# Expert-value tiles 70 to 127 multiplied in three products of split halves

## The chip, the cores and the metric

One Trainium2 chip, one of its cores. The kernel is launched once and computes the whole output. The metric is device time in microseconds (us). Before the change the median of three runs is 2919.87 us (2919.39 to 2923.93).

## The reference

Two transformer blocks run one after the other on 512 tokens of width 1024, all in float32. The first has sliding-window attention, spatial gating and a mixture of 32 experts; the second has a convolution, forgetting attention and a feed-forward layer that picks, for each token, 16 experts out of 16384 in each of 8 heads. The change touches that last layer alone:

```python
u = peer_u[ec]                                   # 128 chosen rows of each token
a = gelu(einsum("ckd,cd->ck", u, hc)) * gc       # a factor for each
vv = peer_v[ec]
out = einsum("ck,ckd->cd", a, vv)                # weighted sum of rows of peer_v
```

`peer_u` and `peer_v` have 16384 rows of 1024 numbers each. The result is added to the tokens, and a last norm follows.

## The kernel before, in words

`peer` (from line 1463) computes this layer in two ways at once, beside each other.

**Gathered half.** For the first 256 tokens (two tiles of 128, `GT`) the chosen rows are fetched one expert slot at a time: `row` (line 1795) has GpSimd issue an indirect DMA that brings one row of 4 KB to each of the 128 partitions (line 1797). There are twelve such buffers (`rtile`). `dots` (line 1804, VectorE) multiplies a fetched row of `peer_u` with the token. `v_sum` adds up four fetched row sets of `peer_v` at a time on TensorE, by weights in `wz` (copied on ScalarE at line 1821; matmuls at line 1825). One such sum stands for four gathers, and it frees four of the twelve buffers. After the 32 sums of a token tile `last_norm` (lines 1834 to 1841) adds the tokens, norms and stores; it runs on VectorE and ScalarE.

**Dense half.** For the other 256 tokens (`DT`) every expert is computed. `u_tile` multiplies one of 128 tiles of `peer_u` (128 experts) with all 256 tokens and writes gelu of it as a slot of 128x256 factors. `gates` (lines 1731 to 1770) builds the gate of each expert and token out of one-hot tiles in batches of 8 tokens, on VectorE (lines 1759 to 1764) and TensorE (line 1748), and multiplies the slots by it on VectorE (line 1752, one instruction for each stretch of slots that lies in one tile). It runs in three parts: experts' tiles 0 to 15, 16 to 79 and 80 to 127. The last part is spread over the steps of V tiles 34 to 79. `v_tile` (line 1772) loads one tile of `peer_v` (512 KB, four buffers, issued by SyncE at line 1490) and multiplies it by its slot: four float32 matmuls at line 1776, for two token tiles and two halves of 512 columns, each recorded as two matmuls. All 128 V tiles add into four banks of PSUM.

There are 94 slots (`NS`); slot i holds tiles i and i+94. The first 50 (`NA`) lie in `big`, the other 44 in `big2`, which is made when U tile 50 is reached. After V tile 69 the slots 50 to 69 hold nothing that is needed any more, since no tile above 127 comes.

**Order.** The loop at line 1886 goes through a list of 256 steps: U tiles 0 to 93, then V and U tiles in turn, then V tiles 34 to 127 alone. After each step it emits a share of the gate batches and, by `fill`, about 2.3 gathers with the sums that go with them. Each engine executes its instructions in the order in which they are emitted.

Elsewhere in the kernel matmuls are made of three products: `split` (line 81) lets ScalarE copy a float32 tile into a rounded half `hi` of type float32r (line 83), and VectorE subtract it for `lo` (line 84); `mm3` (lines 136 to 138) then multiplies hi by hi, hi by lo and lo by hi. Both are used unchanged by the change.

Of the kernel before, what the change touches and what calls it, by code (L numbers as in the profile page):

```python
# [8 lines left out]
F32 = mybir.dt.float32  # L9
F32R = mybir.dt.float32r  # L10
# [10 lines left out]
S, D, NT, KD = 512, 1024, 4, 8  # L21
# [10 lines left out]
class Kern:  # L32
# [1430 lines left out]
    def peer(self):  # L1463
        nc, tc, A = self.nc, self.tc, self.A
        tt, ts, stt = nc.vector.tensor_tensor, nc.vector.tensor_scalar, nc.vector.scalar_tensor_tensor
        act = nc.scalar.activation
        GT, DT, DW = (0, 1), (2, 3), 256
        NS, NA = 94, 50
        parts = [0, 16, 80, 128]
        TB = 8  # L1470
        GS = 32768.0
        with ExitStack() as ctx:
            pb = ctx.enter_context(tc.tile_pool(name="pb", bufs=1, reuse_waits="tile"))
# [4 lines left out]
            def pu(shape=(128, 512)):  # L1478
                return pp.tile(list(shape), F32, tag="u", name=self.nm("pu"), bufs=2)

            def pw(shape=(128, 512)):
                return pp.tile(list(shape), F32, tag="w", name=self.nm("pw"), bufs=4)
# [4 lines left out]
            def load(src, shape):  # L1487

                raw = wp.tile([128] + shape, F32, tag="raw", name=self.nm("raw"))
                nc.sync.dma_start(raw[:], src)  # L1490
                return raw
# [9 lines left out]
            gp = [pb.tile([128, DW], F16, name=f"gp{j}") for j in range(2)]  # L1501
            hd = [pb.tile([128, 4, DW], F32, name=f"hd{j}") for j in range(2)]
            lctx = ctx.enter_context(ExitStack())
            lv = lctx.enter_context(tc.tile_pool(name="plv", bufs=1, reuse_waits="tile"))
            v = [lv.tile([128, 8, 2, 16], F32, name=f"pv{t}") for t in range(NT)]
            ix = [lv.tile([128, 8, 2, 16], U32, name=f"pix{t}") for t in range(NT)]
# [101 lines left out]
            with ExitStack() as c2:  # L1608
# [12 lines left out]
                for t in range(NT):  # L1621
                    tb = slice(t * 128, t * 128 + 128)
                    for j in range(2):
                        x = self.xn[t][j]
# [48 lines left out]
            def picks():  # L1673
# [9 lines left out]
                for t in DT:  # L1683
# [10 lines left out]
                    gT = wk.tile([128, 128], F32, tag="gT", name=self.nm("gT"))  # L1694
                    ts(gT[:], p[:, 2, :], GS, None, op0=OP.mult)
                    nc.vector.tensor_copy(gp[0][:, sl], gT[:])
# [9 lines left out]
            big = [bp.tile([128, NA, DW], F32, name="big")]  # L1706

            def slots(n0, n1):

                while n0 < n1:  # L1710
                    i = n0 % NS
                    b, i, w = (0, i, NA) if i < NA else (1, i - NA, NS - NA)
                    m = min(n1, n0 + w - i)
                    yield n0, m, big[b], i
                    n0 = m

            def slot(n):
                _, _, b, i = next(slots(n, n + 1))
                return b[:, i, :]

            def u_tile(n):

                p = pu()
                raw = load(A["peer_uT"][n].rearrange("p (k e) -> p k e", k=8), [8, 128])
                for k in range(KD):
                    self.u_last = nc.tensor.matmul(p[:, :DW], raw[:, k, :], hd[k // 4][:, k % 4, :], start=k == 0,  # L1726
                                                   stop=k == KD - 1)
                self.gelu = act(slot(n), p[:, :DW], AF.Gelu_apprx_tanh)  # L1728
                self.pace = self.u_last

            def gates(n0, n1, psum):

                w, g = n1 - n0, TB // 2

                def by2(x, t0, w):
                    return x[:, t0:t0 + TB].rearrange("p (g i) -> p g i", i=2)[:, :, None, :].to_broadcast([128, g, w, 2])

                made = []  # L1740

                def products():
                    t0, o2, og = made.pop(0)
                    p = psum([128, TB, w])
                    with tc.issue_after(self.pace.ins):
                        for i in range(TB):
                            for j in range(2):
                                nc.tensor.matmul(p[:, i, :], o2[:, i // 2, :, i % 2], og[j][:, i // 2, :, i % 2], start=j == 0,  # L1748
                                                 stop=j == 1)
                    for n, m, b, i in slots(n0, n1):  # L1750
                        b = b[:, i:i + m - n, t0:t0 + TB]
                        stt(b, p[:, :, n - n0:m - n0].rearrange("p t n -> p n t"), 1.0 / GS, b, op0=OP.mult, op1=OP.mult)  # L1752

                for t0 in range(0, DW, TB):
                    if len(made) == 2:
                        products()
                    o2 = ga.tile([128, g, 128, 2], F16, tag="o2", name=self.nm("o2"), bufs=3)
                    eq = ga.tile([128, g, w, 2], F16, tag="eq", name=self.nm("eq"))
                    tt(o2[:], io[:, None].to_broadcast([128, g, 128, 2]), by2(e2b, t0, 128), op=OP.is_equal)
                    tt(eq[:], io[:, None, n0:n1].to_broadcast([128, g, w, 2]), by2(e1b, t0, w), op=OP.is_equal)  # L1760
                    og = []
                    for j in range(2):
                        o = ga.tile([128, g, w, 2], F16, tag=f"og{j}", name=self.nm("og"), bufs=3)
                        tt(o[:], eq[:], by2(gp[j], t0, w), op=OP.mult)
                        og.append(o)
                    made.append((t0, o2, og))
                    yield
                while made:
                    products()
                    yield  # L1770

            def v_tile(n, acc):
                raw = load(A["peer_v_2"][n * 128:n * 128 + 128, :], [D])
                a = slot(n)
                for t, c in itertools.product(range(2), range(2)):
                    self.pace = nc.tensor.matmul(acc[t][c][:], a[:, t * 128:t * 128 + 128], raw[:, c * 512:c * 512 + 512],  # L1776
                                                 start=n == 0, stop=n == 127)

            def rest_of_big():
                lctx.close()  # L1780
                bq = ctx.enter_context(tc.tile_pool(name="pbig2", bufs=1, reuse_waits="tile"))
                big.append(bq.tile([128, NS - NA, DW], F32, name="big2"))


            ga_t = [ga.tile([128, 128], F32, name=f"ga{t}") for t in GT]
# [78 lines left out]
            def fill(n):  # L1864
                with tc.issue_after(self.pace.ins):
                    while n > 0:
                        k = next(units, None)
                        if k is None:
                            return 0.0
                        n -= k  # L1870
                return n
# [11 lines left out]
            acc, gt, todo, room = None, None, 0, 0.0  # L1883
            nbatch = DW // TB

            for j, (kind, n) in enumerate(seq):
                if kind == "v" and n == 0:
                    acc = [[pw() for _ in range(2)] for _ in range(2)]
                if kind == "v" and n in parts and gt is not None:
                    for _ in gt:  # L1890
                        pass
                    gt = None
                if kind == "u":
                    if n == NA:
                        for _ in picks:
                            pass
                        rest_of_big()
                    if n % 3:
                        next(picks, None)
                    u_tile(n)  # L1900
                else:
                    v_tile(n, acc)
                if gt is not None:
                    todo += rate
                    while todo >= 1:
                        todo -= 1
                        next(gt, None)
                if (kind, n) in start:
                    i = start[kind, n]
                    gt, todo = gates(parts[i], parts[i + 1], pu if i else pw), 0.0  # L1910

                    rest = seq.index(("v", parts[i])) - j - 1
                    rate = (nbatch + 2) / (rest - 1)

                room = fill(room + (1.4 if acc is None and n < NA else 2.3))
# [90 lines left out]
```

## Time and profile before

| | |
|---|---|
| median of three runs | 2919.87 us |
| profiled execution | 2930.82 us |
| its span | 2929.1 us |
| TensorE busy | 2717.2 us (93%) |
| VectorE busy | 1848.5 us (63%) |
| ScalarE busy | 1019.7 us (35%) |
| GpSimd busy | 723.5 us (25%) |
| moved by DMA | 752.10 MB, mean 257 GB/s |

The profiled execution takes 1.7 us more than its span, and 10.95 us more than the median. Shares of busy time are means over the whole span, and its stages have different limits, so the stretch that the change touches has to be read by itself, by windows cut at its own steps. Times in the rows are microseconds from the span's start; PE is TensorE, PEld its weight loads, DVE VectorE, ACT ScalarE, POOL GpSimd, SP SyncE. The "PEclk" column is the granted TensorE clock as a share of 2.4 GHz. "DMA share" is the mean share in which the core's 16 DMA engines had packets under way; packets overlap, so it can pass 1.

### The profile page before, as it was taken

The page shows a single profiled execution, that of the slowest core. Times are in us where ns is not written, and L with a number is a line of the kernel's source. Part 1 is how long each engine was busy: PE and PEld are TensorE (multiplying, and loading weights), DVE is VectorE, ACT ScalarE, POOL GpSimd, SP SyncE. Part 2 cuts the span into 40 slices and gives each one's busy share as a digit, 9 for nine tenths or more (in the row PEclk, how much of TensorE's full clock was granted, in tenths as well). Part 3 has the DMA queues.
Part 4 walks back from the last instruction along what each step waited for, and adds up shares of the span by engine and source line. Part 5 has one row for each costly group of instructions (what it writes and reads, how often), then busy time and mean ns, then how long its engine had stood idle before and what let it go on. Part 6 is the DMA issues. An engine that isn't in the chain of part 4 may idle for free.

```text
span 2929.1 us, 38343 instructions
## 1 busy us (share of the span) xinstructions
PE 2717.2 (93%) x13730; PEld 1907.3 (65%) x13730; DVE 1848.5 (63%) x3907; ACT 1019.7 (35%) x1672; POOL 723.5 (25%) x679
## 2 busy tenths in 40 slices
PE   7999969999999879999999889989989898699998
PEld 4776757777777667766678778877745554244333
DVE  5562569998888858998535399968557522452001
ACT  5442348777777653445633332200100000000000
POOL 1000050000000110101000343566543444444440
PEclk9999979999999989999999999999999999899999
DMA  7226568989999842322222348899988899999995
GB/s 258 87 86 215 206 212 324 355 319 354 351 351 348 317 148 86 108 72 66 89 91 94 119 166 284 335 409 409 360 326 318 327 362 350 324 355 360 369 375 184
DMA packets 228689, 752.10 MB, mean 257 GB/s; under 512 B 28160, under 2 KB 28448, under 8 KB 228496
## 3 DMA queue, kind: packets, MB, share of 16 engines
q1 hardware_dynamic: 145936, 458.69, 43.7%
q0 software_dynamic: 81984, 289.89, 27.1%
q8 instruction: 109, 1.79, 0.3%
q10 hardware_dynamic: 576, 1.05, 0.1%
q14 instruction: 84, 0.69, 0.1%
HBM read 736.90 MB, written 16.81 MB: 257 GB/s over the span
## 4 chain that ended last, share of the span: by engine, by line
PE 40%; DVE 9%; DMA 7%; issue 6%; POOL 2%; ACT 1%; DVEq 0%; another core or an unknown queue 0%; POOLq 0%; SPq 0%; ACTq 0%
PE pw L1776 12%; DMA u<-in_peer_u_dram,ei 6%; PE pu L1726 4%; PE pm L136 4%; PE pm L138 4%; PE pm L137 4%; PE pr L1825 3%; POOL u L1797 2%; DVE u L1804 2%; PE pa L1305 2%; DVE cv L1236 1%; PE pu L1748 1%; PE po L1334 1%; PE pw L138 1%; PE pw L136 1%
## 5 line engine op out<-in xcount | busy, mean ns | idle before, releaser
L84 DVE TENSOR_TENSOR lo<-raw,hi 128x1024 fp32r<-128x1024 f32 (+1 forms) x580 | 624.4, 1107 | 234.3 <-ACT hi L83 214.0
L83 ACT ACTIVATE hi<-raw 128x1024 fp32r<-128x1024 f32 (+1 forms) x600 | 556.9, 952 | 445.1 <-PE pm L137 197.0
L1804 DVE CUSTOM_DVE_ANT_0 u<-u,h 128x1024 f32<-128x1024 f32 x256 | 311.3, 1226 | 305.3 <-DMA u<-in_peer_u_dram,ei 258.7
L1726 PE MATMUL pu<-hd,raw 128*128 128x256 f32 x2048 | 474.1, 390 | 17.4 <-issue 8.3
L1776 PE MATMUL pw<-raw,big 128*128 128x512 f32 x1024 | 471.4, 609 | 6.7 <-DVE big L1752 6.7
L1726 PEld LDWEIGHTS pu<-hd,raw 128*128 128x128 f32 x2048 | 394.3, 195 | 94.9 <-issue 30.2
L1776 PEld LDWEIGHTS pw<-raw,big 128*128 128x128 f32 x1024 | 191.2, 193 | 252.7 <-issue 244.0
L1797 POOL DMA_INDIRECT u<-in_peer_v_dram,eT x256 | 259.2, 1012 | 378.5 <-DVE ga L1804 210.1
L1797 POOL DMA_INDIRECT u<-in_peer_u_dram,ei x256 | 288.4, 1126 | 204.7 <-issue 54.3
L1728 ACT ACTIVATE big<-pu 128x256 f32<-128x256 f32 x128 | 48.9, 384 | 492.6 <-PE pu L1726 430.8
L137 PE MATMUL pm<-lo,xth 128*128 128x512 f32 x512 | 204.8, 400 | 6.5 <-DVE lo L84 6.5
L136 PE MATMUL pm<-hi,xth 128*128 128x512 f32 x512 | 202.1, 395 | 0.0
L138 PE MATMUL pm<-hi,xtl 128*128 128x512 f32 x512 | 201.3, 393 | 0.0
L1236 DVE SCALAR_TENSOR_TENSOR cv<-z,cols,cv 128x496 f32<-128x496 f32 (+27 forms) x240 | 167.2, 735 | 0.5
L905 POOL DMA_INDIRECT yd<-y,idx x16 | 27.6, 1726 | 540.1 <-DVE y L1009 536.6
L138 PE MATMUL pm<-hT,lo 128*128 128x512 f32 x384 | 151.2, 395 | 0.0
L136 PE MATMUL pm<-hT,hi 128*128 128x512 f32 x384 | 151.1, 394 | 0.0
L137 PE MATMUL pm<-hT,hi 128*128 128x512 f32 x384 | 151.0, 393 | 0.0
L1821 ACT ACTIVATE wz<-aT 128x4 f32<-128x4 f32 x64 | 12.8, 209 | 396.9 <-PE pr L1825 396.8
L1825 PE MATMUL pr<-u,wz 128*32 128x512 f32 x1024 | 126.4, 612 | 8.3 <-DMA u<-in_peer_v_dram,eT 8.3
L137 PEld LDWEIGHTS pm<-lo,xth 128*128 128x128 f32 x512 | 96.4, 188 | 40.3 <-DVE lo L84 19.7
L1748 PEld LDWEIGHTS <-o 128*128 128x128 f16 x1536 | 55.0, 98 | 87.5 <-DVE big L1752 43.2
(575 smaller groups left out, 4323.8 us busy)
## 6 DMA issues: line engine op xcount, KB each, us to landing
raw<-in_w_gate_dram SPq DMA_DIRECT2D x128, 512.0 KB
raw<-in_w_up_dram SPq DMA_DIRECT2D x128, 512.0 KB
raw<-in_w_down_dram SPq DMA_DIRECT2D x128, 512.0 KB
raw<-in_peer_uT_dram SPq DMA_DIRECT2D x128, 512.0 KB
raw<-in_peer_v_dram SPq DMA_DIRECT2D x128, 512.0 KB
raw<-in_w_in_dram SPq DMA_DIRECT2D x104, 256.0 KB
wa<-in_w_ada_dram SPq DMA_DIRECT2D x48, 512.0 KB
raw<-in_w_in_dram SPq DMA_DIRECT2D x28, 512.0 KB
```

The costliest lines, as they stand in the source:

```text
L83: return (self.nc.scalar.activation(hi, src, AF.Copy), (eng or self.nc.vector).tensor_tensor(lo, src, hi.bitcast(F32), op=OP.subtract))
L84: (eng or self.nc.vector).tensor_tensor(lo, src, hi.bitcast(F32), op=OP.subtract))
L136: mm(ps, a[0], b[0], start=first, stop=False, **kw)
L137: mm(ps, a[0], b[1], start=False, stop=False, **kw)
L138: return mm(ps, a[1], b[0], start=False, stop=last, **kw)
L1236: stt(a[:, d:], z[:, :512 - d], self.col("conv_w", k * 31 + j), a[:, d:], op0=OP.mult, op1=OP.add)
L1726: self.u_last = nc.tensor.matmul(p[:, :DW], raw[:, k, :], hd[k // 4][:, k % 4, :], start=k == 0, stop=k == KD - 1)
L1748: nc.tensor.matmul(p[:, i, :], o2[:, i // 2, :, i % 2], og[j][:, i // 2, :, i % 2], start=j == 0, stop=j == 1)
L1776: self.pace = nc.tensor.matmul(acc[t][c][:], a[:, t * 128:t * 128 + 128], raw[:, c * 512:c * 512 + 512], start=n == 0, stop=n == 127)
L1797: nc.gpsimd.indirect_dma_start(out=u[:], out_offset=None, in_=A[src], in_offset=bass.IndirectOffsetOnAxis(ap=idx, axis=0))
L1804: nc.vector.tensor_tensor_reduce(u[:], u[:], h3[t][:], scale=1.0, scalar=0.0, op0=OP.mult, op1=OP.add, accum_out=ga_t[t][:, s:s + 1])
L1825: m = nc.tensor.matmul(acc[c][32 * g:32 * g + 32, :], w[:, g, 31 - r:63 - r], us[g][:, c * 512:c * 512 + 512], start=r == 0, stop=r == 31, ...
```

## The change

V tiles below 70 are multiplied as before. From tile 70 on, `v_split` loads the tile, splits it into `vh` and `vl` (128x1024 each) and the slot of factors into `ah` and `al` (128x256 each), and `v_three` multiplies them with `mm3`: four times three float32r matmuls. The split of tile n+1 is emitted ahead of the matmuls of tile n. The four halves have two buffers each, 20 KB in each partition altogether, in a pool that is opened when tile 70 is reached, where slots 50 to 69 lay: `big2` becomes two tiles, slots 50 to 69 and slots 70 to 93 (`big3`), and the first is closed then. `slots` therefore knows three stretches instead of two. The check that all gates of a part are done comes one tile earlier from tile 70 on.

```diff
+        V3 = 70
+            self.b2ctx = ctx.enter_context(ExitStack())
...
-                    b, i, w = (0, i, NA) if i < NA else (1, i - NA, NS - NA)
+                    b = 0 if i < NA else 1 if i < V3 else 2
+                    i, w = i - (0, NA, V3)[b], (NA, V3 - NA, NS - V3)[b]
...
+            def v_split(n):
+
+                raw = load(A["peer_v_2"][n * 128:n * 128 + 128, :], [D])
+                vh, vl, ah, al = [self.vp.tile([128, w], F32R, tag=x, name=self.nm(x), bufs=2)[:] for x, w in (
+                    ("vh", D), ("vl", D), ("ah", DW), ("al", DW))]
+                self.split(ah, al, slot(n))
+                self.split(vh, vl, raw[:])
+                return vh, vl, ah, al
+
+            def v_three(n, acc, x):
+                vh, vl, ah, al = x
+                for t, c in itertools.product(range(2), range(2)):
+                    e, d = slice(t * 128, t * 128 + 128), slice(c * 512, c * 512 + 512)
+                    self.pace = self.mm3(acc[t][c][:], (ah[:, e], al[:, e]), (vh[:, d], vl[:, d]), n == 0, n == 127)
...
-                bq = ctx.enter_context(tc.tile_pool(name="pbig2", bufs=1, reuse_waits="tile"))
-                big.append(bq.tile([128, NS - NA, DW], F32, name="big2"))
+                bq = ctx.enter_context(tc.tile_pool(name="pbig3", bufs=1, reuse_waits="tile"))
+                b3 = bq.tile([128, NS - V3, DW], F32, name="big3")
+                bq = self.b2ctx.enter_context(tc.tile_pool(name="pbig2", bufs=1, reuse_waits="tile"))
+                big.extend([bq.tile([128, V3 - NA, DW], F32, name="big2"), b3])
...
-                if kind == "v" and n in parts and gt is not None:
+
+                if kind == "v" and n + (n >= V3) in parts and gt is not None:
...
+                elif n < V3:
+                    v_tile(n, acc)
                 else:
-                    v_tile(n, acc)
+                    if n == V3:
+                        self.b2ctx.close()
+                        self.vp = ctx.enter_context(tc.tile_pool(name="pv3", bufs=1, reuse_waits="tile"))
+                        nx = v_split(n)
+                    cur, nx = nx, v_split(n + 1) if n < 127 else None
+                    v_three(n, acc, cur)
```

## Rows read from the trace of the kernel before

**Rows 1.** The page: busy time of each engine, its share of the span, instructions.

```profile
PE 2717.2 (93%) x13730; PEld 1907.3 (65%) x13730; DVE 1848.5 (63%) x3907; ACT 1019.7 (35%) x1672; POOL 723.5 (25%) x679
```

**Rows 2.** Windows cut at V tiles 0, 16, 70, 80, 115, end.

```profile
core 0: us, PE busy (x) PEld busy (x) DVE busy (x) ACT busy (x) POOL busy (x), PEclk, DMA share, GB/s
...
2125.64:2312.09 186.45, 157.41 (x1058) 96.85 (x1056) 123.32 (x276) 8.43 (x26) 74.53 (x76) 0.95 0.88 316
...
2663.92:2713.60 49.68, 49.68 (x295) 20.56 (x291) 12.27 (x35) 1.05 (x5) 19.72 (x21) 1.00 0.97 363
2713.60:2874.80 161.20, 161.20 (x604) 59.90 (x600) 0.64 (x1) 3.57 (x17) 70.90 (x78) 1.00 0.98 370
2874.80:2919.70 44.90, 44.90 (x108) 19.68 (x104) 4.01 (x9) 3.19 (x10) 0.00 (x0) 1.00 0.37 126
```

**Rows 3.** Groups by line on TensorE, window 2713.60 to 2874.80.

```profile
L1776 PE MATMUL pw<-raw,big 128*128 128x512 f32 x280 | 125.5, 600 | 0.0
L1825 PE MATMUL pr<-u,wz 128*32 128x512 f32 x324 | 39.1, 598 | 0.0
```

**Rows 4.** TensorE's timeline: the last sum of gathered rows, then V tiles alone.

```profile
2872.95 1.92 PE L1825 MATMUL pr<-u,wz 128*32 128x512 f32 x16
2874.80 44.90 PE L1776 MATMUL pw<-raw,big 128*128 128x512 f32 x104
```

**Rows 5.** TensorE's timeline, experts: first and last of 24 float32r matmuls.

```profile
904.59 0.39 PE L138 MATMUL pm<-hi,xtl 128*128 128x512 f32 x1
...
909.86 0.39 PE L137 MATMUL pm<-lo,xth 128*128 128x512 f32 x1
```

**Rows 6.** Groups by form: splits (600-1000 us), gelu, gate multiplies (2125-2312 us).

```profile
L83 ACT ACTIVATE hi<-raw 128x1024 fp32r<-128x1024 f32 x262 | 263.0, 1053 | 32.6 <-PE pm L138 26.2 <-DMA raw<-in_w_down_dram 4.4 <-DMA raw<-in_w_up_dram 0.7
...
L84 DVE TENSOR_TENSOR lo<-raw,hi 128x1024 fp32r<-128x1024 f32 x263 | 306.9, 1220 | 30.3 <-ACT hi L83 29.2
...
L1728 ACT ACTIVATE big<-pu 128x256 f32<-128x256 f32 x40 | 15.4, 385 | 243.8 <-PE pu L1726 222.7 <-issue 16.3 <-PE pw L1748 4.8
...
L1752 DVE SCALAR_TENSOR_TENSOR big<-pu,big 128x272 f32<-128x272 f32 x31 | 13.4, 434 | 1.7 <-PE pu L1748 1.6
...
L1752 DVE SCALAR_TENSOR_TENSOR big<-pu,big 128x240 f32<-128x240 f32 x31 | 12.3, 397 | 0.0
```

**Rows 7.** DMA, 2663.92 to 2864 us; GpSimd's timeline: the last gather.

```profile
DMA packets 20367, 74.24 MB, mean 371 GB/s; under 512 B 2268, under 2 KB 2268, under 8 KB 20356
...
2852.11 0.94 POOL L1797 DMA_INDIRECT u<-in_peer_v_dram,eT  x1 [0.30 <-issue]
```

**Rows 8.** DMA of GpSimd's queue, 2864 to 2866 us: packets, MB, share.

```profile
q0 software_dynamic: 55, 0.17, 21.4%
```

**Rows 9.** Windows: dot products with U tiles, sums (columns of rows 2).

```profile
1900.00:2050.00 150.00, 135.17 (x846) 116.47 (x845) 111.94 (x241) 13.94 (x40) 103.66 (x80) 0.94 1.03 409
2713.60:2852.00 138.40, 138.40 (x517) 51.59 (x514) 0.00 (x0) 3.57 (x17) 66.71 (x71) 1.00 0.99 371
```

**Rows 10.** Timelines of VectorE and ScalarE: the norm behind the last sum.

```profile
2874.16 1.47 DVE L1837 TENSOR_TENSOR xe<-xe,pr 128x512 f32<-128x512 f32 x2 [161.69 <-PE pr L1825]
...
2877.16 1.41 DVE L1840 SCALAR_TENSOR_TENSOR xo<-xe,rs,gf 128x512 f32<-128x512 f32 x2
...
2876.61 0.30 ACT L203 ACTIVATE rs<-ss,eps 128x1 f32<-128x1 f32 x1 [0.23 <-DVE ss L202]
```

**Rows 11.** VectorE's timeline: the dense norm's second add.

```profile
2918.03 0.69 DVE L1837 TENSOR_TENSOR xe<-xe,pw 128x512 f32<-128x512 f32 x1 [0.17 <-PE pw L1776]
```

**Rows 12.** Gathers (2713-2852, 2100-2350, 1900-2050 us by form; whole span by line).

```profile
L1797 POOL DMA_INDIRECT u<-in_peer_v_dram,eT x71 | 66.7, 940 | 75.8 <-PE pr L1825 56.0 <-issue 14.5 <-PE pw L1776 5.3
...
L1797 POOL DMA_INDIRECT u<-in_peer_v_dram,eT x55 | 56.9, 1034 | 105.4 <-DVE ga L1804 99.5 <-DVE eq L1760 2.7 <-issue 2.3
...
L1797 POOL DMA_INDIRECT u<-in_peer_u_dram,ei x69 | 92.2, 1336 | 32.2 <-issue 16.4 <-DMA u<-in_peer_u_dram,ei 12.8 <-DVE og L1764 3.0
...
L1797 POOL DMA_INDIRECT u<-in_peer_v_dram,eT x256: 935/939/1982, 2018.6 to 2852.1; - x128
```

## Prediction, made before the changed kernel was run

> **What bounds the kernel now.** The page's first table shows TensorE busy for 2717.2 us of the span [rows 1]: the engine to relieve, but a share over the whole span says nothing of one stage. So the second view is windows cut at the steps that the change touches [rows 2]. V tile 70 starts at 2663.92 us. In the 49.68 us up to tile 80, in the 161.20 us up to tile 115 and in the 44.90 us of the last 13 tiles alone TensorE is busy all the time at full clock, 2.4 GHz: in these 255.8 us every microsecond taken from TensorE could come off the end. The same rows carry the warning. In the first two windows the DMA share is 0.97 and 0.98, with 363 and 370 GB/s; only behind the last sum does it fall to 0.37. I call these two windows the mixed stretch (210.9 us) and the third the tail.
>
> The third view, groups by line, shows what fills the mixed stretch: V tiles (280 records, eight a tile, so 35 tiles from tile 80 on) and sums of gathered rows (324 records, 16 a sum) [rows 3]. With the ten tiles before, it holds 45 V tiles and, by the sums that the trace counts there, 26 sums. Each sum waits for four gathers, and each V tile for its 512 KB. So a shorter TensorE helps in the mixed stretch only as far as transfers can follow; in the tail it helps in full.
>
> **The matmuls.** The tail takes 44.90 us for 13 tiles [rows 4], 3.45 us each. A new tile has twelve float32r matmuls. In the experts 24 such matmuls of the same shape, bound by nothing else, start from 904.59 to 909.86 us [rows 5]: 5.27 us for 23 steps, 0.229 us each. Twelve make 2.75 us, and a tile saves 0.70 us. Neither row holds a wait, so no range is needed here. The Trainium skill, page "FP8 and Floating Point Precision", section "TensorE Precision Notes", counts four passes for a true float32 matmul, by which three products would take three quarters, 2.59 us as an estimate: 0.11 us a tile less than measured here for the same instructions, some 1.4 us in the tail.
>
> **The splits.** Each tile adds on ScalarE a copy of 128x1024 (1.053 us) and one of 128x256 (0.385 us, the gelu of that shape), on VectorE a subtraction of 128x1024 (1.220 us) and one of 128x256 (0.397 us by the nearest row, 128x240) [rows 6]. That is 1.44 and 1.62 us per tile; beside a tile of 2.75 us it fits, and both engines are nearly idle in the mixed stretch (ScalarE 4.62 us, VectorE 12.91 us in 210.9 us, rows 2 added). The halves have two buffers, so the split of tile n+2 waits until tile n is multiplied, and has only tile n+1's matmuls as cover. The way from the end of tile n to `vl` of n+2 is 0.385 + 1.053 + 1.220 us and three handoffs of at most 0.23 us, the one that the norm's row shows [rows 10]: between 2.66 and 3.35 us. The second product of n+2 needs it 2.75 + 0.23 = 2.98 us after. Two tiles then take that way plus 2.52 us of products, so the step is between 2.75 (covered) and 2.94 us; I take 2.85. Where a sum of 1.85 us (2872.95 to 2874.80 [rows 4]) stands between, it is covered. Tiles 70 to 79 have gate work ahead of the subtraction on VectorE, 12.27 us for ten tiles [rows 2]; if the cover is gone, a tile loses up to 1.2 us, and tiles with a sum beside them lose nothing. I take 2 us for all ten, between 0 and 12.
>
> **The switch at tile 70.** The new buffers lie where slots 50 to 69 were, so the first split waits for tile 69's matmuls, and nothing covers it: 2.66 us, up to 3.35. The gathers run on meanwhile. A pair of loads is not added: SyncE loads the same tiles through the same four buffers, now freed by the splits, a tile earlier.
>
> **The norm behind the last sum.** `last_norm` for the second token tile stands in VectorE's and ScalarE's queues ahead of the split of tile 116. VectorE is in it from 2874.16 until 2878.57 us, 4.6 us behind the sum's last product near 2874.0; ScalarE until 2876.91 [rows 10]. The subtractions need another 1.6 us, so `vl` of tile 116 comes some 6 us after the sum, and TensorE, with one tile ready (2.75 us and a product of 0.23), stands still for 3 us; now it has only V tiles there and waits for nobody. Between 0 (if that norm is emitted a step later) and 6; I take 3.
>
> **The mixed stretch, as TensorE sees it.** 210.9 us less 45 times 0.70 (31.5), plus 2.7 for the switch and 2 for the gates: 184.1 us.
>
> **The mixed stretch, as transfers see it.** From tile 70's start to 2864 us 74.24 MB move at 371 GB/s; the last gather is issued at 2852.11 [rows 7] and q0's packets have thinned out to 0.17 MB in the 2 us from 2864 on [rows 8]. Its sum starts at 2872.95, so gathers now run 9 us ahead of TensorE. That lead is used up first if TensorE becomes faster than its rows. What is unknown is the rate when the queues never run dry. The trace has it at 409 GB/s, with 1.03 of the engines' share, for 150 us in which the same gathers ran beside tiles of the same size; in the sums' stretch it is 371 at 0.99 [rows 9]. So the ends are 371 (the engines have no more to give with this mix) and 409. I take 400, nearer the upper one: it has the same two queues and sizes, and waiting packets are what the change makes. 74.24 MB then take 185.6 us, and with 1 us for the landing and 1.85 for the last sum the stretch is 188.5 us, longer than TensorE's 184.1: transfers set its end, and it saves 22.4 us. At 409 it is 184.4 us (26.5 saved), at 371 it is 203.0 us (7.9 saved).
>
> **The tail.** Of 13 tiles the last counts half, because the norm's first adds start at 2918.03 us, within it [rows 11]: 12.5 times 0.60 (3.45 less 2.85) is 7.5 us, less 3 for the norm: 4.5. What follows the last tile is unchanged.
>
> **Earlier.** Tiles 16 to 79 now lie in three pieces, so each of 32 gate batches has three multiplies on VectorE where it had two. They take 434 + 397 ns for 272 and 240 numbers a partition [rows 6]; for 272, 160 and 80 the same line gives about 434 + 320 + 240, 0.16 us more, 5.2 us in all. In that window VectorE works 123.32 of 186.45 us [rows 2], and the rest, waits for rows, covers most. I take 1, between 0 and 5.
>
> **The sum.** 22.4 + 4.5 - 1 = 25.9 us: 2930.82 becomes 2904.9 for the profiled execution, and against the median, 10.95 us below it, 2919.87 becomes 2894.0. A measurement of this kernel can tell about 0.2% (5.8 us) from no change.
>
> **The rivals.**
> *The transfers give nothing more.* At 371 GB/s the mixed stretch saves 7.9 us, the whole 7.9 + 4.5 - 1 = 11.4: 2908.5. For it: the share is 0.99 already. Against it: 409 for 150 us. The Trainium skill's "DMA: Bandwidth & Descriptors", section "Where 436 GB/s comes from", puts the HBM side at about 358 GB/s per core as what binds loads; the trace disagrees, with 409 and 371. Chance 0.17.
> *TensorE stays the bound and the covers hold.* At 409 GB/s, with no gate, norm or handoff stall: 31.5 - 2.7 saved in the stretch is more than transfers allow, so 26.5 + 12.5 times 0.70 = 35.3: 2884.6. Chance 0.08.
> *Little or nothing is left.* 371 GB/s, the norm's stall at 6 us, the gates' extra work uncovered: 7.9 + 7.5 - 6 - 5 = 4.4, within 0.2%: 2915.5. Chance 0.08.
> *Slower: the subtractions hold up GpSimd's gathers.* A gather takes 0.940 us with VectorE idle, 1.034 and 1.336 us where VectorE runs two-operand products and other work, at most 1.982 [rows 12], plus 0.30 us between two [rows 7]. A sum has 210.9/26 = 8.11 us now; four gathers pass that from 1.73 us a gather on. If every gather met a subtraction and took 1.98, four would take 9.1 us, 26 sums 26 us more, and with the tail 26 - 4.5 + 1 = 22.5 slower: 2942. Against it: VectorE is busy 112 of 150 us where the mean is 1.336 [rows 9, 12], and the new work is 1.6 us in some 4. The Trainium skill, "SBUF — State Buffer", section "Who interferes with whom", says that a VectorE instruction with two SBUF inputs contends with a GpSimd instruction that reads SBUF; the subtraction is one, and the trace shows a loss of 0.09 to 0.4 us a gather beside such work. Chance 0.07.
> The forecast itself has 0.60. That the products are not the cheap ones can be ruled out: the type and shape are those of rows 5.
>
> **The numbers.** 2894 us. The range reaches from a little under the second rival (2884.6) to the first with its earlier gate work uncovered too (2908.5 + 4): 2882 to 2912; what it leaves out is the third and the fourth, and some of the second. Faster by over 0.2%: the forecast, the first two rivals, 0.85, less a little of the first's upper end: 0.82. Within 0.2%: 0.10. Slower: 0.08. TensorE's clock is in these: where it was busy for 157.41 of 186.45 us it had 0.95 [rows 2], and a wait of a few per cent in the mixed stretch may cost some of that.
>
> **What would show it.** The windows after should have V tiles of twelve matmuls, 2.75 to 2.95 us in the tail; a mixed stretch near 188 us with DMA at 400 GB/s and TensorE waiting for gathered rows or raw tiles; one gap of 2.7 us at tile 70 and one of 3 us after the last sum. Wrong would be: waits of TensorE for `vl` at every tile, a rate still at 371 with a share near 1 (first rival), or gathers of over 1.7 us on GpSimd (the slower one).

## The result and the profile after

The changed kernel takes 2890.66 us (median of four runs, 2888.25 to 2899.49) against 2921.77 us before (four runs, the three from above and one more): a ratio of 0.9899, with a 95% interval from 0.9876 to 0.9922. That is 31 us less, where 26 were forecast, inside the range of 2882 to 2912.

The two profiled executions differ by more: their spans are 2929.1 and 2886.5 us, 42.6 us apart. So the first thing to read is where in the span the difference lies. These are windows of the changed kernel, cut at the same steps as [rows 2] (V tiles 70, 80, 115 and the last one's end; same columns):

```profile
2653.14:2696.57 43.43, 43.37 (x329) 27.18 (x329) 28.88 (x56) 15.93 (x27) 20.73 (x20) 1.00 1.02 400
2696.57:2839.20 142.63, 139.26 (x745) 85.80 (x741) 57.61 (x70) 51.45 (x87) 79.37 (x78) 0.99 1.03 409
2839.20:2876.78 37.58, 36.55 (x160) 28.96 (x156) 23.33 (x31) 17.78 (x31) 0.00 (x0) 1.00 0.54 191
```

The mixed stretch went from 49.68 + 161.20 = 210.88 us to 43.43 + 142.63 = 186.06 us, the tail from 44.90 to 37.58 us. Together that is 32.1 us, near the 31 us between the medians. The other 10 us lie ahead of tile 70, which starts at 2653.14 us for 2663.92: experiment 1 shows that single executions scatter there by more than that, so they can't be put down to the change. Two columns changed with the time: transfers went from 363 and 370 to 400 and 409 GB/s, with the engines' share at 1.02 and 1.03; and TensorE, busy without a break before, has 3.4 us of idle time among sums and tiles. All that it waited for on the way, by the view of waits (waiter, what ended it: us in total, times, the longest):

```profile
PE pr L1845 <- DMA u<-in_peer_v_dram,eT: 3.4, 3, 2.3
PE pw L136 <- ACT vh L83: 1.1, 1, 1.1
PE pw L137 <- DVE vl L84: 1.0, 1, 1.0
```

Three waits for gathered rows, one for `vh` (the switch at tile 70) and one for `vl` (the norm behind the last sum). In 58 tiles there is no wait on a split's round but those two.

### The profile page after: what moved, and what is told of

It reads as the page before. It is cut to its first block, busy times and chain, and to the rows that moved or that the text cites. A ratio compares the mean times of both kernels' runs of the same rounds, so it can differ in the third digit from the quotient of the medians.

```text
span 2886.5 us, 39245 instructions
## 1 busy us (share of the span) xinstructions
PE 2676.6 (93%) x13962; PEld 1946.1 (67%) x13962; DVE 1943.7 (67%) x4055; ACT 1099.6 (38%) x1788; POOL 738.7 (26%) x679
## 4 chain that ended last, share of the span: by engine, by line
PE 40%; DVE 9%; DMA 7%; issue 5%; POOL 2%; ACT 1%; DVEq 0%; POOLq 0%; ACTq 0%; SPq 0%
PE pu L1729 5%; PE pw L1794 5%; DMA u<-in_peer_u_dram,ei 5%; PE pm L136 4%; PE pm L138 4%; PE pm L137 4%; PE pr L1845 4%; PE pw L136 2%; PE pw L137 2%; PE pw L138 2%; DVE u L1824 2%; POOL u L1817 2%; DMA u<-in_peer_v_dram,eT 2%; PE pa L1305 2%; DVE cv L1236 1%
## 5 line engine op out<-in xcount | busy, mean ns | idle before, releaser
L1817 POOL DMA_INDIRECT u<-in_peer_v_dram,eT x256 | 272.9, 1066 | 346.1 <-DVE ga L1824 203.9
L1794 PE MATMUL pw<-raw,big 128*128 128x512 f32 x560 | 262.8, 614 | 3.2 <-DVE big L1755 3.2
L1794 PEld LDWEIGHTS pw<-raw,big 128*128 128x128 f32 x560 | 105.1, 195 | 131.2 <-issue 126.1
L136 PEld LDWEIGHTS pm<-hi,xth 128*128 128x128 f32 x512 | 96.3, 188 | 21.1 <-ACT xth L83 0.2
```

The source lines that it names most:

```text
L136: mm(ps, a[0], b[0], start=first, stop=False, **kw)
L1817: nc.gpsimd.indirect_dma_start(out=u[:], out_offset=None, in_=A[src], in_offset=bass.IndirectOffsetOnAxis(ap=idx, axis=0))
```

## The experiments

The first four take the change apart. Beside each of the eleven, the kernel before ran on the same chip.

**1. Only the three pieces.** All V tiles keep the float32 matmuls; the slots lie in three tiles.

```diff
-                elif n < V3:
+                elif n < 128:
                     v_tile(n, acc)
...
             while next(units, None) is not None:
                 pass
+            self.b2ctx.close()
```

> The slots lie in three tiles and the pool stays open, but all 128 V tiles are multiplied as before, so nothing is left of the change but a third gate multiply in each of 32 batches. My theory of the early part: 0 to 5.2 us slower than before, about 1 us. Rival, from the two profiles (tile 70 starts 10.8 us earlier after the change): the new layout itself gains there, and this kernel is some 10 us faster than before.

Measured: 2920.89 us (ten runs) against 2922.99, ratio 0.9995, interval 0.9982 to 1.0008. The third piece costs nothing that can be measured, and the 10 us that the rival gives the layout lie outside the interval (some 5 us faster to 2 us slower). Yet in its profiled execution the time from V tile 0 to tile 70 was 521.0 us, where the first profile of the kernel before had 538.3 (row one, this kernel; row two, the one before; windows):

```profile
2120.10:2641.13 521.03, 469.07 (x2546) 252.56 (x2545) 261.77 (x601) 23.54 (x76) 241.26 (x241) 0.96 0.94 348
```

```profile
2125.64:2663.92 538.28, 474.72 (x2547) 256.25 (x2545) 260.91 (x569) 23.58 (x76) 238.87 (x241) 0.95 0.92 338
```

Two executions with the same work there, but for 32 gate multiplies more on VectorE in the quicker one, lie 17 us apart. What makes one of them slower stays open. A difference of that size ahead of tile 70 between two single profiles therefore says nothing; the mixed stretch, by contrast, has 210.97 and 210.88 us.

**2 and 3. Only the tail, only the mixed stretch.**

```diff
# experiment 2
-                elif n < V3:
+                elif n < 115:
                     v_tile(n, acc)
...
-                    if n == V3:
+                    if n == 115:
# experiment 3
-                elif n < V3:
+                elif n < V3 or n >= 115:
                     v_tile(n, acc)
...
-                    cur, nx = nx, v_split(n + 1) if n < 127 else None
+                    cur, nx = nx, v_split(n + 1) if n < 114 else None
```

> Only tiles 115 to 127, behind the last sum, are multiplied in three products. If the tail pays by itself what the profiles show (44.90 us became 37.58 us), and the switch now falls into it (1.5 to 2.7 us), this is 4.5 to 6 us faster than before. If the tail's gain hangs on the mixed stretch ahead of it, it is 0 to 2 us.

> Only tiles 70 to 114 are multiplied in three products, the last 13 as before. By the profiles the mixed stretch went from 210.9 to 186.1 us, so some 25 us faster than before, 2897. If the gain there were partly the luck of one profiled execution, 15 us or less.

Measured: the tail alone has a ratio of 0.9970 (0.9956 to 0.9984), some 9 us of 2922; the mixed stretch alone 0.9926 (0.9909 to 0.9943), some 22 us. The two add up to the whole change (0.9899). By the runs alone (5 to 13 us) the tail could still have given the 6 us that I expected at most; by its profile it gave more, 35.7 us for 37.6 in the full change, since the switch at tile 115 is hidden beside the last sum and the norm's stall falls out.

**4. The splits without their use.** From tile 70 on everything is split, and the products are the old ones.

```diff
-                return vh, vl, ah, al
+                return raw, slot(n)
...
-                    self.pace = self.mm3(acc[t][c][:], (ah[:, e], al[:, e]), (vh[:, d], vl[:, d]), n == 0, n == 127)
+                    self.pace = nc.tensor.matmul(acc[t][c][:], a[:, e], raw[:, d], start=n == 0, stop=n == 127)
```

> From tile 70 on everything is split as in the change, but the halves are not used: the matmuls are the old float32 ones, from the raw tile and the slot. It shows what the splits cost by themselves. My theory: they are covered, so 0 to 3 us slower than before (the third piece, and loads that wait for TensorE again). Rival (subtractions hold up the gathers on GpSimd): the mixed stretch grows by more than 10 us.

Measured: ratio 0.9995 (0.9981 to 1.0010). Windows of tiles 70 to 79 and 80 to 114, and the gathers by form in the second:

```profile
2647.96:2697.73 49.77, 49.77 (x296) 20.42 (x291) 30.66 (x62) 18.23 (x33) 22.87 (x21) 1.00 0.97 359
2697.73:2858.93 161.20, 161.20 (x604) 59.89 (x601) 59.22 (x79) 53.66 (x95) 77.91 (x78) 1.00 0.98 371
```

```profile
L1817 POOL DMA_INDIRECT u<-in_peer_v_dram,eT x70 | 72.8, 1040 | 68.5 <-PE pr L1845 52.4 <-issue 13.7 <-PE pw L1788 2.4
```

VectorE now works 59.22 us in the window where it worked 0.64, ScalarE 53.66 where it worked 3.57 [rows 2], and the window is 161.20 us long, to the hundredth what it was. The subtractions do slow the gathers, from 0.940 [rows 12] to 1.040 us each (0.94 for the 29 beside which VectorE stood still, 1.11 for the other 41), 0.4 us for a sum's four. GpSimd is still idle for 68.5 us there, and 52.4 of them end with a sum that frees its buffers, so nobody notices. The slower rival is out.

The next three ask what sets the end of the mixed stretch. My prediction said transfers; the small waits speak for TensorE.

**5. Two products.** The product of `al` and `vh` is left out.

```diff
-                    self.pace = self.mm3(acc[t][c][:], (ah[:, e], al[:, e]), (vh[:, d], vl[:, d]), n == 0, n == 127)
+                    nc.tensor.matmul(acc[t][c][:], ah[:, e], vh[:, d], start=False, stop=False)
+                    self.pace = nc.tensor.matmul(acc[t][c][:], ah[:, e], vl[:, d], start=False, stop=n == 127)
```

> Leaves out the third product (lo of the factors by hi of the tile): eight matmuls a tile, 1.82 us where twelve take 2.72. If transfers set the end of the mixed stretch at 409 GB/s, as I predicted, it stays at 182 to 185 us (186.1 with three products) and only the tail gains, down to the split's own round of 2.3 to 2.4 us a tile: 6 to 8 us faster than the changed kernel, about 2883. If TensorE sets it and rows merely follow, all 58 tiles gain 0.9 us: 40 to 50 us faster than the changed kernel, about 2845.

**6. Half loads.** From tile 70 on 512 of 1024 columns are loaded and stand for both halves.

```diff
-                raw = load(A["peer_v_2"][n * 128:n * 128 + 128, :], [D])
+                raw = load(A["peer_v_2"][n * 128:n * 128 + 128, 0:512], [512])
...
-                self.split(vh, vl, raw[:])
+                two = raw[:, None, :].to_broadcast([128, 2, 512])
+                vh2, vl2 = [x.rearrange("p (a d) -> p a d", a=2) for x in (vh, vl)]
+                self.split(vh2, vl2, two)
```

> From tile 70 on only the first 512 columns of each V tile are loaded (256 KB for 512) and used for both halves: the same instructions on all engines, 15 MB less to move. Both theories: TensorE's waits for rows (3.4 us) go and the stretch is what TensorE needs, 180 to 183 us, so 3 to 6 us faster than the changed kernel. If transfers weighed more than the waits show, over 10 us faster.

**7. Both of these edits.**

> Both cuts: eight matmuls a tile and half of each V tile loaded. TensorE then needs 45 times 1.82 plus 26 times 1.87 plus 7, some 138 us in the mixed stretch; transfers need 61 MB at 409 GB/s, some 150 to 153 us. If transfers are the wall behind TensorE, the stretch ends at about 153 us, 33 us less than in the changed kernel, with the tail's 6: about 2851. If something else (the split's round, GpSimd's issue of gathers) stands there, it is 165 us or more: 2863 or above.

Measured: two products 2868.13 us (0.9825, interval 0.9795 to 0.9855), half loads 2882.84 (0.9877, 0.9843 to 0.9910), both 2841.35 (0.9727, 0.9695 to 0.9758). The intervals of half loads and of the change (0.9899) overlap, so what tells these two apart is the profiles. Windows of half loads over the whole mixed stretch, and of the changed kernel over the same:

```profile
2652.52:2833.42 180.90, 180.83 (x1068) 112.84 (x1068) 87.13 (x127) 67.39 (x114) 98.75 (x98) 1.00 0.98 360
```

```profile
2653.14:2839.20 186.06, 182.63 (x1069) 112.98 (x1069) 86.49 (x125) 67.38 (x114) 100.10 (x98) 0.99 1.03 407
```

With half loads TensorE is busy without a break, so 180.90 us is what it needs for these tiles and sums; in the changed kernel transfers add 5.2 us to that. Now two products, from tile 70 to the last sum (window; waits; DMA until the last gather has landed):

```profile
2645.17:2840.86 195.69, 169.07 (x958) 95.61 (x958) 98.89 (x145) 81.38 (x134) 105.10 (x98) 0.96 1.03 409
```

```profile
PE pr L1846 <- DMA u<-in_peer_v_dram,eT: 26.6, 18, 3.9
```

```profile
DMA packets 21631, 78.89 MB, mean 409 GB/s; under 512 B 2399, under 2 KB 2399, under 8 KB 21618
```

Here TensorE waits 26.6 us for gathered rows, and transfers run at 409 GB/s for the whole stretch: the 78.89 MB until the last gather has landed take 193 us, and the last sum starts 195.7 us after tile 70. With half the tile loads as well, that stretch is 31.7 us shorter: the waits shrink by 22.8 us, to 3.8, and TensorE is busy for 8.9 us less, at a granted clock of 1.00 for 0.96:

```profile
2657.26:2821.28 164.02, 160.19 (x959) 93.95 (x959) 98.64 (x145) 81.44 (x134) 106.67 (x98) 1.00 1.02 398
```

So transfers are a wall at 409 GB/s, and it stands right behind TensorE. My numbers for experiments 5 (2883) and 7 (2851) missed by 15 and 10 us, and that is not against the wall: I had kept the order. The order on TensorE is settled when the kernel is built. It is not the order in which the instructions are emitted (the text on the kernel before says that it is): they are emitted alike in experiment 5 and in the change, and yet with shorter tiles the sums were put further apart. 21 of the last 26 stand ahead of tile 115, the last after tile 125, where in the change it stands after tile 114. From tile 70 to the end of tile 127 experiment 5 saves 21 us (202.3 us for 223.6), not the 53 that 58 tiles of 0.91 us would give; experiment 7, with less to move, takes 170.6 us there and saves those 53. From tile 70 on, experiments 5 and 7 have the same order, matmul for matmul, so those two compare directly, and so do 6 and the change.

**8. Gathers spread out.** If DMA is the wall in the mixed stretch and has room in the tail (191 GB/s), the gathers might go there.

```diff
-                room = fill(room + (1.4 if acc is None and n < NA else 2.3))
+                room = fill(room + (1.4 if acc is None and n < NA else 2.2))
```

> 2.2 gathers a step are emitted for 2.3, so they reach to V tile 123 for 113 and transfers are less dense in the mixed stretch. If transfers set its end, the stretch and the tail together gain 4 to 8 us over the changed kernel. If TensorE sets it, only the 3.4 us of waits can go: between 3 us faster and, where the early part or the later last norm loses, 5 us slower.

Measured: 2875.22 us (0.9847, 0.9813 to 0.9881), 15 us less than the change where I had expected 8 at most. The waits for rows did not go (5.1 us); mixed stretch and tail together did not gain at all but grew by 10.9 us, from 223.6 to 234.5, 7.4 of them the four sums that moved in; and the time from V tile 0 to tile 70 fell from 528.3 to 502.4 us. That is more than the 17 us by which that stretch scattered in experiment 1, and it is not where I had looked for it.

**9 to 11. The spread without the change, more of it, and the change again.** Experiment 9 is the kernel before with 2.2, experiment 10 the changed one with 2.15, experiment 11 the changed one as it is, all beside each other.

> The kernel before, with 2.2 gathers a step instead of 2.3. My theory of the gain in the spread version of the changed kernel: it comes ahead of tile 70, where fewer gathers and sums stand beside the gates, so it is there without the change too: 10 to 16 us faster than before, with the mixed stretch unchanged at its pace. Rival: it needs the room that the three products make at the end, and this kernel is within 5 us of before.

> The changed kernel with 2.15 gathers a step, so the last sum falls at tile 127. If fewer gathers ahead of tile 70 keep paying, 3 to 6 us faster than with 2.2 (2870). If the norm behind the last sum then comes after the last tile and is no longer covered, it is 0 to 6 us slower than with 2.2 (2875 to 2881).

> The changed kernel once more, beside the other two on one chip: 0.9899 of before, between 0.988 and 0.992.

Measured: 2900.45 us (0.9928, 0.9907 to 0.9950), 2871.24 (0.9836, 0.9812 to 0.9860) and 2888.83 (0.9889, 0.9865 to 0.9912). The spread is worth 21 us without the change, more than I had expected, and 14 to 18 with it, so it is a second gain of its own. Window from V tile 0 to tile 70 in the kernel before with the spread, and the wait that is TensorE's longest in total there:

```profile
2127.26:2626.14 498.88, 460.81 (x2482) 252.09 (x2481) 260.25 (x564) 22.84 (x72) 227.42 (x229) 0.97 0.95 351
```

```profile
PE pu L1748 <- DVE big L1752: 26.5, 8, 7.6
```

The two profiles under experiment 1 have 538.3 and 521.0 us there; 7.4 us of the difference are the four sums that now come behind tile 70. In the first profile of the kernel before that wait, gate products that wait for VectorE's gate multiplies, is 38.0 us with a longest of 17.2. In the profiles of the change and of experiments 1 and 11, with 2.3 gathers a step too, it is 38.6 to 40.4 us; in experiments 8 and 10 it is 30.6 and 32.9. It points to VectorE, whose queue has dot products waiting for rows ahead of the gates; that chain was read, not tried. Between 2.2 and 2.15 there is no difference to be measured: tile 127 ends 8.8 us earlier in the profile with 2.15, but the last norm then comes after it (17.3 us from the end of tile 127 to the end of the span, for 9.8), which takes most of that back. Both lie below the changed kernel: 2.15, run beside it, by intervals that do not touch; 2.2, run on another chip, by intervals that overlap a little.

## Why the prediction was right

**The matmuls.** Right. In the tail a tile takes 2.72 us from start to start (V tiles 118 to 127) where it took 3.43; I had 2.75. That is 0.71 us saved, and 0.68 in the mixed stretch (210.88 less 180.90 us with half loads, plus 0.44 for the switch, by 45 tiles), where I had 0.70 for both. The prediction's 2.59 us, counted by passes, lies 0.16 us below its 2.75 and not 0.11, which makes 2.1 us in the tail and not 1.4; nothing was added up from it.

**The splits.** Covered, as said; experiment 4 shows it for the engines, the waits for the round. The round of two tiles was too dear: I took 2.85 us a tile for 2.72. The gate work at tiles 70 to 79, for which I took 2 us, costs nothing that shows: with half loads a tile saves 0.67 us there and 0.68 from tile 80 on. ScalarE and VectorE in the tail (timelines):

```profile
2871.15 0.42 ACT L83 ACTIVATE ah<-big 128x256 fp32r<-128x256 f32 x1 [1.35 <-PE pw L137]
2871.47 1.04 ACT L83 ACTIVATE vh<-raw 128x1024 fp32r<-128x1024 f32 x1
```

```profile
2872.55 1.23 DVE L84 TENSOR_TENSOR vl<-raw,vh 128x1024 fp32r<-128x1024 f32 x1 [0.52 <-ACT vh L83]
```

From the start of `ah` to the end of `vl` are 2.63 us, less than my lower bound of 2.66: the handoffs hide in the overlap of one instruction's end with the next one's start. The 0.23 us of a norm's tiny instruction do not apply.

**The switch.** 1.65 us, against 2.66: tile 69 to 70 took 5.15 us where it took 3.94 with the same gate work, and tile 70 to 71 0.44 more than the old step less 0.73. Only the 0.44 fall into the mixed stretch, as it is cut. One timeline row tells why (TensorE, tile 70):

```profile
2653.14 1.20 PE L136 MATMUL pw<-vh,ah 128*128 128x512 f32 x4 [1.05 <-ACT vh L83]
```

All four products that need only `ah` and `vh` were put first, so TensorE works while `vl` is made.

**The norm behind the last sum.** 1.9 us, against 3. The steps from tile 116 are 3.19 and 4.14 us where 2.72 is the pace. I had the whole norm ahead of the split of tile 116 on VectorE; in the built kernel that split stands between the norm's two adds, and it is `vl` of tile 117 that comes too late:

```profile
2840.57 0.69 DVE L1857 TENSOR_TENSOR xe<-xe,pr 128x512 f32<-128x512 f32 x1 [2.48 <-DMA xe<-x3d]
2841.18 1.22 DVE L84 TENSOR_TENSOR vl<-raw,vh 128x1024 fp32r<-128x1024 f32 x1
2842.31 0.68 DVE L1857 TENSOR_TENSOR xe<-xe,pr 128x512 f32<-128x512 f32 x1
```

The first add also waited 2.48 us for the norm's own load of tokens (`xe`), which I had not counted. It starts 1.4 us after the sum's end; with half loads (experiment 6) it starts 0.6 us before the sum's end, and the two steps are 2.72 and 3.11 us (VectorE's timeline there):

```profile
2832.78 0.69 DVE L1859 TENSOR_TENSOR xe<-xe,pr 128x512 f32<-128x512 f32 x1 [0.45 <-PE pr L1847]
```

So 1.5 of the 1.9 us go away where transfers have room. My 3 us also counted from 2874.0, near which the first half of the sum was done; its last product ended at 2874.87 [rows 4].

With the two sizes the tail is right: 44.90 less 13 times 0.71 plus 1.9 is 37.6 us, measured 37.58; I had 40.4. The half tile that I left out comes behind it: from the end of tile 127 to the end of the span are 9.75 us where 9.40 were.

**The mixed stretch.** The size was near (188.5 predicted, 186.06 measured), the reason half wrong. The step that failed is "transfers set its end". TensorE alone needs 180.9 us (experiment 6), less than my 184.1: the switch took 0.44 us of the 2.7 in it and the gates nothing of the 2, while the tiles saved 1.1 us less than I had. Transfers, taken at 400 GB/s, ran at 407 over the stretch and at 409 from tile 80 on, my upper end. So the two limits meet: TensorE sets the pace, three waits for rows add 5.2 us, and experiment 5 shows the wall behind. The third of these waits is at tile 103; in the eleven tiles from 104 to 114 no sum waits for its rows, so it is TensorE that ends the stretch. A second profile of the changed kernel (experiment 11) has 186.3 us and three such waits again. That the number held although I had named the other limit is in part luck: by my own sums the two lie less than 5 us apart.

Of the rivals, "371 and no more" and with it "little or nothing" are refuted by the 409 GB/s, and the slower one by experiment 4. "TensorE stays the bound and the covers hold" was nearer to the mechanism than my forecast: TensorE is the bound, and the covers hold at every tile but the two beside the norm; what it lacked is the norm's 1.9 us. The Trainium skill's "DMA: Bandwidth & Descriptors", section "Where 436 GB/s comes from", with its 358 GB/s, does not fit this core: 409 held for 195 us. The Trainium skill's section "Measured" on the same page, with 425 GB/s for 16 MB on a core alone, is nearer.

**Earlier.** The third piece costs nothing that can be measured (experiment 1) where I put 1. In the profiles the stretch saved 24.8 us where I had 22.4, and the tail 7.3 where I had 4.5. The split into parts was thus right to 3 us in each, and both errors went the same way.

## What to carry to other kernels

Where one stage has two resources near their limit, cut each alone and then both: one number (the 180.9 us with half the loads, the 409 GB/s with two products) says how far the other limit is, and what the next cut can bring. Compare stages by windows cut at the same steps and check with an unchanged stage how much a single execution scatters; here one early stretch moved by 17 us by itself, while the stretch under study repeated to 0.1 us with the old matmuls (experiments 1, 2, 4 and before) and to 0.7 us with the new ones (experiments 3, 11 and the change). And when gathers run beside work that fills the engines, try their rate first: one constant was worth 21 us on the old kernel, nearly as much as the mixed stretch of this change.

## What was not expected of the hardware

A wait of 2.27 us for rows cost 3.9 us. Window of the sum behind that wait, and its row on TensorE's timeline:

```profile
2793.08:2796.60 3.52, 3.52 (x17) 0.59 (x17) 0.16 (x1) 0.00 (x0) 0.94 (x1) 0.52 1.02 407
```

```profile
2793.08 3.59 PE L1845 MATMUL pr<-u,wz 128*32 128x512 f32 x16 [2.27 <-DMA u<-in_peer_v_dram,eT]
```

The granted clock fell to 0.52, about the lower level of 1.2 GHz, and the sum took 3.59 us where others take 1.92; the next products were at full pace again. The sums behind the two other waits of the stretch, of 0.87 and 0.23 us, took 1.92 us like the rest. That is how 3.4 us of waits became 5.1 of the 5.2. The second profile (experiment 11) has the same at the same tile: a wait of 2.71 us, then a sum of 3.24. The Trainium skill, "TensorE: Matmul & The Clock Gate", section "What's actually happening", describes this drop to half the clock after idle time; the rows agree on the level.
